# A two-layer encoder trunk: transposes through DRAM move to GpSimd's queue in runs of 512 bytes, and the last piece of y is transposed on TensorE

## The chip, the cores and the metric

The kernel runs on one core of one Trainium2 chip. The metric is the device time of one execution in microseconds, the median of several runs. The profile is one further execution, recorded instruction by instruction.

## The reference

Two identical layers act on x of 256 positions by 2048 channels, in float32. In each layer, with h the RMS-normalised input:

```python
u = h @ w_in                 # cq, ckv, kr, az | bq, bk, bv, bz | cq, ck, cv, cz | 3 gates of 2048
# A: latent attention; B: difference of two softmax maps per head; C: attention with a position bias
# q and k are normalised per head and multiplied by a gain; A and B rotate part of them
branches = (o_a * silu(a_z), o_b * silu(b_z), o_c * silu(c_z))      # 1024 channels each
y = sum(sigmoid(gate[n]) * (branches[n] @ w_branch[n]) for n in range(3))
x = x + y @ w_out
```

## The kernel before, in words

All products with weights go through one helper, `matunit` (L138 to L166). It multiplies a left side of 256 positions, stored transposed (channels on partitions), with 512 columns of a weight matrix. The weights come from DRAM as a stream in the order of use: chunks of 256 rows by 512 columns (512 KB), each loaded by SyncE (L153) into one of four buffers, cast on ScalarE to the high part (L154), and subtracted on VectorE to give the low part (L155). Each chunk feeds twelve TensorE matmuls: high by high, high by low and low by high, for two row blocks and two position blocks (L163 to L165). Four PSUM tiles hold two such products at a time.

An operand that was computed with positions on partitions has to be transposed before it can be a left side, and q, k and the branch outputs have to be transposed for attention and the branch projection. There are two ways. `to_transposed` (L199 to L213) uses TensorE: eight 128x128 transposes into PSUM for a piece of 512 channels, and then a split into high and low parts on ScalarE and VectorE, two halves of 128x512. `bounce` (L218 to L230) goes through DRAM. VectorE transposes 32x32 blocks of the piece in place (L223, two instructions), SyncE writes the piece to a DRAM tile (L225, 512 KB), and SyncE reads it back in four DMAs of 128 KB (L229), one for each quarter of the partitions, in runs of 32 floats (128 bytes), so that whole rows stand transposed afterwards. `from_bounced` (L232 to L241) then splits the result: ScalarE writes the high part times a gain, VectorE the low part. The variants `split_stacked` and `split_twice` place the parts of branch B's q and k on both halves of the partitions.

A `bounce` is used 42 times: for the normalised latent cq (once a layer), for the gated halves of A, B and C (six a layer), for q and k of the halves of B and C (eight a layer), for the four pieces of y (four a layer, L663), and for the four pieces of layer 1's input, in layer 0's output projection (L725). The gated halves of A and C are bounced before attention, and `simple_half` (L381 to L396) multiplies each head's output into the bounced tile (L395).

The order of a layer is: the latents, A in two halves, B in two halves, then the gates and the branch projection of A (`gate_branch(0)`), C in two halves, `gate_branch(1)` for B, `gate_branch(2)` for C, and the output projection. `gate_branch(2)` finishes y piece by piece (j = 0 to 3, L647 to L663), and the output projection reads all four pieces in each of its products (L712). Before it, GpSimd issues the load of the residual `xres` (2 MB, L703), whose buffer is that of `yacc`, the sum of y; in layer 0 GpSimd also issues the writes of the new x to DRAM (L721).

GpSimd computes the inverse roots of the norms (`rstd`, L245 and L246), the products behind them (L267, L424), and the rotary products of B's q and k and of A's shared key (L282 to L287, L552); it issues the loads of C's bias (L675). VectorE then scales and transposes what GpSimd has finished.

Every engine executes its instructions in order, and each queue of DMA issues is in order too. The order on each engine isn't written out by hand: a planner places the instructions of all engines by its own estimates of their times, starting from the order of the program. Two pools matter for the change: `zp` has four buffers of the tag z, for the gated halves and the tile that the pieces of y are read back to (L662), and `ps_t` has two PSUM buffers for transposes.

Of the kernel before, what the change touches and what calls it, by code (L numbers as in the profile page):

```python
# [14 lines left out]
P = 128  # L15
# [6 lines left out]
HH = 4  # L22
# [59 lines left out]
def trunk_kernel(ctx: ExitStack, tc: tile.TileContext, x, xT, w, cols, rows, tab, bias, ident_d, out):  # L82
# [106 lines left out]

    def split_twice(d0, d1, l0, l1, src, gain):  # L190

        a, b = slice(0, 64), slice(64, P)
        for hi, lo, d, dl in ((a, b, d0, l0), (b, a, d1, l1)):
            for o in (hi, lo):
                nc.scalar.activation(d[o], src[hi], AF.Copy, scale=gain[hi])
                nc.vector.scalar_tensor_tensor(out=dl[o], in0=src[hi], scalar=gain[hi],
                                               in1=d[hi].bitcast(F32), op0=ALU.mult, op1=ALU.subtract)

# [19 lines left out]
    def bounce(src, name, dst=None):  # L218


        dst = src if dst is None else dst
        for t in range(NT):
            nc.vector.transpose(dst[:, t, :], src[:, t, :])  # L223
        scr = dram.tile([SEQ, 512], F32, name=f"{name}_scr")
        nc.sync.dma_start(scr.rearrange("(t p) f -> p t f", p=P), dst)  # L225
        sv = scr.rearrange("(i r) (b j c) -> j r b i c", r=32, b=HH, j=4, c=32)
        flat = dst.rearrange("p t f -> p (t f)")
        for j in range(4):
            nc.sync.dma_start(flat[32 * j:32 * j + 32].rearrange("p (b i c) -> p b i c", b=HH, c=32), sv[j])  # L229
        return flat.rearrange("p (b q) -> p b q", b=HH)  # L230

    def from_bounced(z, dh, dl, gain, per_block=False, put=None):  # L232

        if put is not None:
            for b0 in (0, 2):
                put(slice(b0, b0 + 2), z[:, b0:b0 + 2, :])
        elif per_block:
            for b in range(HH):
                split(dh[:, b, :], dl[:, b, :], z[:, b, :], gain(b))
        else:  # L240
            split(dh, dl, z, gain)  # L241

# [138 lines left out]
    def simple_half(z, parts, v, add, name):  # L381

        zt = bounce(z, f"{name}zT")
        for hl in range(HH):
# [9 lines left out]
            o = attend_transposed(p, v, hl, n)  # L394
            nc.vector.tensor_tensor(out=zt[:, hl, :], in0=o[:, :SEQ], in1=zt[:, hl, :], op=ALU.mult)  # L395
        return zt  # L396
# [38 lines left out]
    for l in range(DEPTH):  # L435
# [135 lines left out]
        def b_split(z, hf, name, gain=None):  # L571
            bh[hf] = zp.tile([P, HH, SEQ], F32R, tag=f"bh{hf}", name=f"{name}h", bufs=1)
            bl[hf] = zp.tile([P, HH, SEQ], F32R, tag=f"bl{hf}", name=f"{name}l", bufs=1)
            split(bh[hf], bl[hf], z, gain)

# [35 lines left out]
        for hf in range(2):  # L611
            n = f"l{l}b{hf}"
            op = {}
            for i, nm in ((1, "k"), (0, "q")):
# [5 lines left out]
                if nm == "k":  # L620
                    d = [att_tile(f"{n}{nm}{m}") for m in range(2)]
                    put = lambda bs, pt: split_twice(d[0][:, 0, bs, :], d[1][:, 0, bs, :], d[0][:, 1, bs, :],
                                                     d[1][:, 1, bs, :], pt, cg[:, 4:5])
                else:
                    d = att_tile(f"{n}{nm}")
                    d = [d[:, 0], d[:, 1]]
                    put = lambda bs, pt: split_stacked(d[0][:, bs, :], d[1][:, bs, :], pt, cg[:, 1:2])
                from_bounced(bounce(nat, f"{n}{nm}T"), None, None, None, put=put)
                op[nm] = d
# [14 lines left out]
        def gate_branch(n):  # L644
            for j in range(4):
# [13 lines left out]
                if n == 2:  # L659
                    yt = att_tile(f"{nm}y")  # L660
                    yh[j], yl[j] = yt[:, 0], yt[:, 1]
                    yz = zp.tile([P, NT, 512], F32, tag="z", name=f"{nm}yz")  # L662
                    from_bounced(bounce(yacc[:, :, js], f"{nm}yT", yz), yh[j], yl[j], None)  # L663

# [140 lines left out]
```

## Time and profile before

| | us |
|---|---|
| median of 3 runs | 2031.13 |
| lowest and highest run | 2028.79, 2031.28 |
| the profiled execution: its own time | 2029.23 |
| the profiled execution: its span, first to last instruction | 2027.3 |

| engine | busy share of the span | instructions |
|---|---|---|
| TensorE matmul | 98% | 9112 |
| VectorE | 63% | 1750 |
| ScalarE | 55% | 1624 |
| GpSimd | 11% | 357 |

Times in the rows below are counted from the start of the span. PE is TensorE's matmul row, PEld its weight loads, DVE is VectorE, ACT ScalarE, POOL GpSimd, SP SyncE; a q behind the name is that engine's sequencer. A matmul's recorded length (0.39 us) overlaps the next one's, so the distance of their starts is read, not the length. PEclk is the granted share of the full TensorE clock. Names give layer and place: l0o is layer 0's output projection, l0n2j3y the last piece of y, l0b1q the q of B's second half. A tile that ends in `T_scr` is a bounce's tile in DRAM.

### The profile page before, as it was taken

Reading aid. Unit: us, or ns where it says so; the run is one execution under the profiler, and the core shown is the slowest. Engines: PE = TensorE matmul, PEld = TensorE weight load, DVE = VectorE, ACT = ScalarE, POOL = GpSimd, SP = SyncE. Lnnn points to the kernel's source line nnn. Section 1 sums busy time; section 2 is a strip of 40 time slices with the busy share of each in tenths; the row PEclk is TensorE's granted clock in tenths of the full one; section 3 lists DMA queues with packets and bytes.
Section 4 is the critical chain, followed back from the end, with each engine's and each line's share of the span. In section 5 each row is a group of like instructions: output and inputs, shape, how many; then the busy total and the mean of one; then the engine's idle time right before and its main releaser. Section 6 shows DMA issues by size and latency. Waiting matters only on the chain.

```text
span 2027.3 us, 25409 instructions
## 1 busy us (share of the span) xinstructions
PE 1985.4 (98%) x9112; PEld 1647.3 (81%) x9112; DVE 1267.4 (63%) x1750; ACT 1107.0 (55%) x1624; POOL 225.4 (11%) x357
## 2 busy tenths in 40 slices
PE   9999999999999999998999999999999999999989
PEld 7888778888888888887888887788888888888867
DVE  5778777545666555555657777775456665555544
ACT  6677667545555544443556766664456564444433
POOL 2313040001000000000023220400010100000000
PEclk9999999999999999999999999999999999999989
DMA  8765565666776656677886665756676676657774
GB/s 295 219 188 175 186 207 187 207 204 209 223 210 212 192 191 197 215 235 241 260 237 205 180 181 173 227 178 209 204 220 214 203 217 189 196 197 211 235 228 156
DMA packets 293325, 421.39 MB, mean 208 GB/s; under 512 B 187328, under 2 KB 191424, under 8 KB 292432
## 3 DMA queue, kind: packets, MB, share of 16 engines
q1 hardware_dynamic: 290992, 410.80, 65.4%
q0 software_dynamic: 1920, 8.46, 1.3%
q8 instruction: 71, 1.16, 0.2%
q14 instruction: 54, 0.44, 0.1%
q10 hardware_dynamic: 288, 0.52, 0.1%
HBM read 393.51 MB, written 26.21 MB: 207 GB/s over the span
## 4 chain that ended last, share of the span: by engine, by line
PE 77%; DMA 8%; ACT 4%; POOL 3%; DVE 3%; issue 3%; SPq 2%; ACTq 0%; POOLq 0%; DVEq 0%
PE l1g_p L164 4%; PE l1g_p L165 4%; PE l1g_p L163 4%; PE l0g_p L164 4%; PE l0g_p L165 4%; PE l0g_p L163 4%; SPq L229 2%; PE l1o_p L163 1%; PE l1o_p L165 1%; PE l1o_p L164 1%; PE l0o_p L164 1%; PE l0o_p L163 1%; PE l0o_p L165 1%; DMA l0cq_r<-w 1%; PE l1az_p L164 1%
## 5 line engine op out<-in xcount | busy, mean ns | idle before, releaser
L155 DVE TENSOR_TENSOR l1g_l<-l1g_r,l1g_h 128x1024 fp32r<-128x1024 f32 x96 | 117.3, 1222 | 94.4 <-ACT l1g_h L154 94.3
L155 DVE TENSOR_TENSOR l0g_l<-l0g_r,l0g_h 128x1024 fp32r<-128x1024 f32 x96 | 117.2, 1222 | 93.3 <-ACT l0g_h L154 93.2
L154 ACT CAST l0g_h<-l0g_r 128x1024 fp32r<-128x1024 f32 x96 | 101.1, 1053 | 130.0 <-PE l0g_p L165 79.8
L154 ACT CAST l1g_h<-l1g_r 128x1024 fp32r<-128x1024 f32 x96 | 101.1, 1054 | 127.8 <-PE l1g_p L165 78.1
L164 PE MATMUL l0g_p<-l0g_l,xh 128*128 128x512 f32 x384 | 149.8, 390 | 0.0
L165 PE MATMUL l0g_p<-l0g_h,xl 128*128 128x512 f32 x384 | 149.7, 390 | 0.0
L164 PE MATMUL l1g_p<-l1g_l,xh 128*128 128x512 f32 x384 | 149.7, 390 | 0.0
L165 PE MATMUL l1g_p<-l1g_h,xl 128*128 128x512 f32 x384 | 149.7, 390 | 0.0
L163 PE MATMUL l1g_p<-l1g_h,xh 128*128 128x512 f32 x384 | 136.0, 389 | 0.0
L163 PE MATMUL l0g_p<-l0g_h,xh 128*128 128x512 f32 x384 | 136.0, 390 | 0.0
L164 PEld LDWEIGHTS l0g_p<-l0g_l,xh 128*128 128x128 f32 x384 | 72.1, 188 | 15.3 <-DVE l0g_l L155 0.5
L164 PEld LDWEIGHTS l1g_p<-l1g_l,xh 128*128 128x128 f32 x384 | 72.1, 188 | 14.8
L165 PEld LDWEIGHTS l1g_p<-l1g_h,xl 128*128 128x128 f32 x384 | 72.1, 188 | 14.7
L165 PEld LDWEIGHTS l0g_p<-l0g_h,xl 128*128 128x128 f32 x384 | 72.1, 188 | 14.7
L163 PEld LDWEIGHTS l0g_p<-l0g_h,xh 128*128 128x128 f32 x384 | 72.1, 188 | 14.7
L163 PEld LDWEIGHTS l1g_p<-l1g_h,xh 128*128 128x128 f32 x384 | 72.0, 188 | 14.7
L155 DVE TENSOR_TENSOR l1o_l<-l1o_r,l1o_h 128x1024 fp32r<-128x1024 f32 x32 | 39.2, 1224 | 46.1 <-ACT l1o_h L154 46.1
L154 ACT CAST l1o_h<-l1o_r 128x1024 fp32r<-128x1024 f32 x32 | 33.7, 1054 | 58.5 <-PE l1o_p L165 45.6
L155 DVE TENSOR_TENSOR l0o_l<-l0o_r,l0o_h 128x1024 fp32r<-128x1024 f32 x32 | 38.8, 1219 | 29.5 <-ACT l0o_h L154 29.5
L154 ACT CAST l0o_h<-l0o_r 128x1024 fp32r<-128x1024 f32 x32 | 33.3, 1051 | 39.5 <-PE l0o_p L165 32.0
L703 POOL DMA_DIRECT2D xres<-x x1 | 0.8, 784 | 309.5 <-DVE l0n2j3yz L223 309.5
L703 POOL DMA_DIRECT2D xres<-xscr x1 | 0.8, 792 | 308.8 <-DVE l1n2j3yz L223 308.8
(1600 smaller groups left out, 5866.3 us busy)
## 6 DMA issues: line engine op xcount, KB each, us to landing
l0g_r<-w SPq DMA_DIRECT2D x96, 512.0 KB, 3.6
l1g_r<-w SPq DMA_DIRECT2D x96, 512.0 KB, 4.2
l0o_r<-w SPq DMA_DIRECT2D x32, 512.0 KB, 4.9
l1o_r<-w SPq DMA_DIRECT2D x32, 512.0 KB, 4.4
l0az_r<-w SPq DMA_DIRECT2D x16, 512.0 KB, 4.7
l1az_r<-w SPq DMA_DIRECT2D x16, 512.0 KB, 4.7
l0b0k_r<-w SPq DMA_DIRECT2D x8, 512.0 KB, 3.7
l0b0q_r<-w SPq DMA_DIRECT2D x8, 512.0 KB, 3.3
```

Source lines behind the costliest of these rows:

```text
L154: state["cast"] = nc.scalar.copy(wh[:, ks, :N], wr[:, ks, :N])
L155: nc.vector.tensor_tensor(out=wl[:, ks, :N], in0=wr[:, ks, :N], in1=wh[:, ks, :N].bitcast(F32), op=ALU.subtract)
L163: nc.tensor.matmul(ps[t][:, :N], h[:, ts], wh[:, k2, :N], start=first, stop=False)
L164: nc.tensor.matmul(ps[t][:, :N], h[:, ts], wl[:, k2, :N], start=False, stop=False)
L165: nc.tensor.matmul(ps[t][:, :N], lo[:, ts], wh[:, k2, :N], start=False, stop=last)
L229: nc.sync.dma_start(flat[32 * j:32 * j + 32].rearrange("p (b i c) -> p b i c", b=HH, c=32), sv[j])
L703: nc.gpsimd.dma_start(xres, x_src.rearrange("(t p) d -> p t d", p=P))
```

## The change

- `bounce` writes VectorE's transposes to a new tile `turned` (a z buffer), in an order in which the four channel blocks of a partition quarter lie together. The DRAM tile holds for each position row four runs of 128 floats, and the four reads fetch runs of 512 bytes. The write and the reads are issued by GpSimd.
- The bounced tile now has the order (position block, head, position in block). `bounced` and `as_bounced` are views that bring it and its targets together, in runs of 32 elements; the splits and the product in `simple_half` go through them.
- `from_bounced` multiplies by the gain in place, in a ScalarE pass of its own over the whole tile, and then splits without a gain; the case of one gain per block is as it was. `split_twice` loses its gain, and `split_stacked` is called without one. Both now take the whole tile at once and not two halves.
- In `gate_branch(2)`, the piece j = 3 goes through `to_transposed`, on TensorE.

```diff
--- before.py
+++ after.py
@@ -187,14 +187,13 @@
                 nc.vector.scalar_tensor_tensor(out=d[lo], in0=src[hi], scalar=gain[hi],
                                                in1=d[hi].bitcast(F32), op0=ALU.mult, op1=ALU.subtract)
 
-    def split_twice(d0, d1, l0, l1, src, gain):
+    def split_twice(d0, d1, l0, l1, src):
 
         a, b = slice(0, 64), slice(64, P)
         for hi, lo, d, dl in ((a, b, d0, l0), (b, a, d1, l1)):
             for o in (hi, lo):
-                nc.scalar.activation(d[o], src[hi], AF.Copy, scale=gain[hi])
-                nc.vector.scalar_tensor_tensor(out=dl[o], in0=src[hi], scalar=gain[hi],
-                                               in1=d[hi].bitcast(F32), op0=ALU.mult, op1=ALU.subtract)
+                nc.scalar.copy(d[o], src[hi])
+                nc.vector.tensor_tensor(out=dl[o], in0=src[hi], in1=d[hi].bitcast(F32), op=ALU.subtract)
 
     def to_transposed(src, nblk, dh, dl, gain, name, per_block=False, put=None):
 
@@ -218,27 +217,42 @@
     def bounce(src, name, dst=None):
 
 
+
+        turned = zp.tile([P, NT, 4, HH, 32], F32, tag="z", name=f"{name}_tu")
+        scr = dram.tile([NT, P, 4, 128], F32, name=f"{name}_scr")
+        for t in range(NT):
+            nc.vector.transpose(turned[:, t].rearrange("p j b c -> p b j c"), src[:, t, :])
+        nc.gpsimd.dma_start(scr.rearrange("t p j f -> p t (j f)"), turned.rearrange("p t j b c -> p t (j b c)"))
         dst = src if dst is None else dst
-        for t in range(NT):
-            nc.vector.transpose(dst[:, t, :], src[:, t, :])
-        scr = dram.tile([SEQ, 512], F32, name=f"{name}_scr")
-        nc.sync.dma_start(scr.rearrange("(t p) f -> p t f", p=P), dst)
-        sv = scr.rearrange("(i r) (b j c) -> j r b i c", r=32, b=HH, j=4, c=32)
         flat = dst.rearrange("p t f -> p (t f)")
+        sv = scr.rearrange("t (i r) j f -> j r (t i) f", r=32)
         for j in range(4):
-            nc.sync.dma_start(flat[32 * j:32 * j + 32].rearrange("p (b i c) -> p b i c", b=HH, c=32), sv[j])
-        return flat.rearrange("p (b q) -> p b q", b=HH)
+            nc.gpsimd.dma_start(flat[32 * j:32 * j + 32].rearrange("p (q f) -> p q f", f=128), sv[j])
+        return flat
+
+    def bounced(z, b=None):
+
+        v = z.rearrange("p (q b c) -> p q b c", b=HH, c=32)
+        return v if b is None else v[:, :, b, :]
+
+    def as_bounced(d):
+
+        if len(d.shape) == 2:
+            return d.rearrange("p (q c) -> p q c", c=32)
+        return d.rearrange("p b (q c) -> p q b c", c=32)
 
     def from_bounced(z, dh, dl, gain, per_block=False, put=None):
 
+        if per_block:
+            for b in range(HH):
+                split(as_bounced(dh[:, b, :]), as_bounced(dl[:, b, :]), bounced(z, b), gain(b))
+            return
+        if gain is not None:
+            nc.scalar.activation(z, z, AF.Copy, scale=gain)
         if put is not None:
-            for b0 in (0, 2):
-                put(slice(b0, b0 + 2), z[:, b0:b0 + 2, :])
-        elif per_block:
-            for b in range(HH):
-                split(dh[:, b, :], dl[:, b, :], z[:, b, :], gain(b))
+            put(bounced(z), as_bounced)
         else:
-            split(dh, dl, z, gain)
+            split(as_bounced(dh), as_bounced(dl), bounced(z))
 
     def rstd(ss, n, width, name):
 
@@ -392,7 +406,8 @@
                 pc = p[:, 0:P] if t == 0 else p[:, P:384]
                 nc.scalar.activation(pc, pc, AF.Copy, scale=su[:, t:t + 1])
             o = attend_transposed(p, v, hl, n)
-            nc.vector.tensor_tensor(out=zt[:, hl, :], in0=o[:, :SEQ], in1=zt[:, hl, :], op=ALU.mult)
+            zc = bounced(zt, hl)
+            nc.vector.tensor_tensor(out=zc, in0=as_bounced(o[:, :SEQ]), in1=zc, op=ALU.mult)
         return zt
 
     def diff_half(z, parts, v, nlam, name):
@@ -571,7 +586,7 @@
         def b_split(z, hf, name, gain=None):
             bh[hf] = zp.tile([P, HH, SEQ], F32R, tag=f"bh{hf}", name=f"{name}h", bufs=1)
             bl[hf] = zp.tile([P, HH, SEQ], F32R, tag=f"bl{hf}", name=f"{name}l", bufs=1)
-            split(bh[hf], bl[hf], z, gain)
+            from_bounced(z, bh[hf], bl[hf], gain)
 
         za = [None, None]
         qr = [None, None]
@@ -619,13 +634,12 @@
                     rope(v, v, rt[:, t, c0:c0 + 16], rt[:, t, c0 + 16:c0 + 32], 8, 8, nc.gpsimd, f"{n}{nm}r{t}")
                 if nm == "k":
                     d = [att_tile(f"{n}{nm}{m}") for m in range(2)]
-                    put = lambda bs, pt: split_twice(d[0][:, 0, bs, :], d[1][:, 0, bs, :], d[0][:, 1, bs, :],
-                                                     d[1][:, 1, bs, :], pt, cg[:, 4:5])
+                    put = lambda pt, v: split_twice(v(d[0][:, 0]), v(d[1][:, 0]), v(d[0][:, 1]), v(d[1][:, 1]), pt)
                 else:
                     d = att_tile(f"{n}{nm}")
                     d = [d[:, 0], d[:, 1]]
-                    put = lambda bs, pt: split_stacked(d[0][:, bs, :], d[1][:, bs, :], pt, cg[:, 1:2])
-                from_bounced(bounce(nat, f"{n}{nm}T"), None, None, None, put=put)
+                    put = lambda pt, v: split_stacked(v(d[0]), v(d[1]), pt)
+                from_bounced(bounce(nat, f"{n}{nm}T"), None, None, cg[:, 1:2] if i == 0 else cg[:, 4:5], put=put)
                 op[nm] = d
             v = vsplit(in_unit(f"b{hf}v"), rcol, f"{n}v")
             zb[hf] = silu_gate(in_unit(f"b{hf}z"), rcol, f"{n}z")
@@ -659,8 +673,11 @@
                 if n == 2:
                     yt = att_tile(f"{nm}y")
                     yh[j], yl[j] = yt[:, 0], yt[:, 1]
-                    yz = zp.tile([P, NT, 512], F32, tag="z", name=f"{nm}yz")
-                    from_bounced(bounce(yacc[:, :, js], f"{nm}yT", yz), yh[j], yl[j], None)
+                    if j < 3:
+                        yz = zp.tile([P, NT, 512], F32, tag="z", name=f"{nm}yz")
+                        from_bounced(bounce(yacc[:, :, js], f"{nm}yT", yz), yh[j], yl[j], None)
+                    else:
+                        to_transposed(lambda t: yacc[:, t, js], 4, yh[j], yl[j], None, f"{nm}yT")
 
         gate_branch(0)
         for hf in range(2):
```

## Rows read from the trace of the kernel before

**Rows 1.** Busy time of the engines, page.

```profile
PE 1985.4 (98%) x9112; PEld 1647.3 (81%) x9112; DVE 1267.4 (63%) x1750; ACT 1107.0 (55%) x1624; POOL 225.4 (11%) x357
```

**Rows 2.** A window in the gates; length, then busy us (instructions) by engine.

```profile
700.00:915.00 215.00, 215.00 (x950) 177.93 (x949) 119.66 (x117) 97.92 (x101) 0.00 (x0) 1.00 0.66 207
```

**Rows 3.** TensorE's waits: total us, times, longest us.

```profile
PE l1o_p L163 <- ACT l1n2j3y L171: 8.0, 1, 8.0
PE l0o_p L163 <- ACT l0n2j3y L171: 6.1, 1, 6.1
PE l0b1v_p L163 <- ACT l0b1v_h L154: 2.4, 1, 2.4
PE l0c_s L311 <- ACT l0c1q L174: 1.6, 1, 1.6
PE l0b0z_p L163 <- ACT l0b0z_h L154: 1.6, 1, 1.6
PE l1b0z_p L163 <- ACT l1b0z_h L154: 1.5, 1, 1.5
...
PE l1az_p L163 <- ACT l1az_h L154: 0.9, 1, 0.9
```

**Rows 4.** Windows behind long waits; third column from the right is the granted clock.

```profile
302.00:305.40 3.40, 3.40 (x9) 2.61 (x10) 2.65 (x3) 0.00 (x0) 0.00 (x0) 0.50 0.55 86
942.30:947.10 4.80, 4.80 (x11) 3.79 (x12) 2.33 (x2) 1.05 (x1) 0.00 (x0) 0.50 0.79 287
1220.20:1227.00 6.80, 6.48 (x16) 5.02 (x17) 6.26 (x15) 2.77 (x6) 0.00 (x0) 0.50 0.48 147
1949.90:1954.00 4.10, 4.10 (x10) 3.23 (x11) 2.32 (x2) 1.03 (x1) 0.00 (x0) 0.50 0.75 272
```

**Rows 5.** The chain that ended last: start us, us, what.

```profile
109.62 0.87 PE l0a0kT_t L205 x8
...
923.02 1.31 DVE l0n2j3yz L223 x2
```

**Rows 6.** Timeline of ScalarE in both output projections; idle time before it in brackets.

```profile
930.81 1.05 ACT L154 CAST l0o_h<-l0o_r 128x1024 fp32r<-128x1024 f32 x1 [1.67 <-PE l0o_p L165]
934.63 1.05 ACT L154 CAST l0o_h<-l0o_r 128x1024 fp32r<-128x1024 f32 x1 [2.76 <-DMA l0o_r<-w]
...
1943.68 1.04 ACT L154 CAST l1o_h<-l1o_r 128x1024 fp32r<-128x1024 f32 x1 [6.17 <-DMA l1o_r<-w]
```

**Rows 7.** Line L229, the reads: issue ns min/median/max.

```profile
L229 SPq DMA_DIRECT2D x1n<-x1T_scr x16: 562/672/2798, 957.4 to 1026.5; - x16
```

**Rows 8.** The chain that ended last, around two read-backs.

```profile
204.68 1.33 SPq L229
...
207.72 4.63 DMA l0b0z_r<-w
...
1048.17 3.04 SPq L229
1053.20 6.34 DMA l1az_r<-w
```

**Rows 9.** Line L721, the writes of x that GpSimd issues: ns min/median/max.

```profile
L721 POOL DMA_DIRECT2D xscr<-xres x4: 727/727/760, 951.4 to 1017.1; - x4
```

**Rows 10.** A window in branch B's second half; the fifth engine is GpSimd.

```profile
271.00:296.10 25.10, 25.10 (x112) 20.79 (x111) 19.57 (x25) 13.41 (x17) 20.64 (x29) 1.00 0.81 234
```

**Rows 11.** DMA issues: queue, count, KB each, median us from issue to landing.

```profile
xscr<-xres POOLq DMA_DIRECT2D x4, 512.0 KB, 4.8
x1T_scr<-x1n SPq DMA_DIRECT2D x4, 512.0 KB, 5.0
```

**Rows 12.** The chain that ended last, a split of C's q.

```profile
629.33 1.16 ACT l0c1q L174
```

**Rows 13.** Timeline of GpSimd in the rotary products of B's second half.

```profile
277.83 0.32 POOL L285 TENSOR_TENSOR l0b1kr_b<-l0b1k_n,rt 128x64 f32<-128x64 f32 x1
...
279.47 1.32 POOL L285 TENSOR_TENSOR l0b1kr_b<-l0b1k_n,rt 128x64 f32<-128x64 f32 x1
```

## The prediction

> **What bounds the kernel now.** I read the page's busy time first: TensorE is busy for 98% of the span [rows 1]. In an undisturbed stretch 950 matmuls take 215 us, 0.226 us each [rows 2], so nearly all the time is matmul issue, which this change hardly touches. Only the holes in TensorE's row can be won or lost, so the second view is the list of TensorE's waits [rows 3]. Two stand apart: each layer's output projection (L163, l0o_p and l1o_p) waits 6.1 and 8.0 us for ScalarE's split of the last piece of y, which has come back from DRAM. The others are 2.4 us or less. Third, the windows with the granted clock [rows 4]: after both long waits TensorE ran at 0.50, the 1.2 GHz level, for 11 matmuls in 4.80 us and 10 in 4.10 us; the same level stands after the l1b0z wait and around the l0b1v wait. Fourth, I asked what ends the short waits.
>
> **The last piece of y.** It leaves the DRAM round trip: no transposes on VectorE, no write, no four reads, no wait for them. Removed are the two waits, 6.1 + 8.0 = 14.1 us, and the matmuls at the lower level: 4.80 - 11 x 0.226 = 2.3 us and 4.10 - 10 x 0.226 = 1.8 us, together 4.1 us [rows 3, 4]. Added are eight TensorE transposes a layer: a group of eight takes 0.87 us, so 1.7 us for both layers [rows 5]. Their source is ready at 923.02, when the old way's VectorE transposes start [rows 5]; TensorE went on at 942.3 after 6.1 us of waiting, so it wants the piece at 936.2, 13 us later. The split, now two halves each on ScalarE and VectorE, has its cover there. Net so far -16.5 us.
>
> **What is late next there: weights.** While the last piece travels, the residual (xres, 2 MB, issued by GpSimd) is loading. A ScalarE cast of a weight chunk normally idles 1.67 us before it, waiting for TensorE; one cast in each layer idled 2.76 and 6.17 us instead, for its weights [rows 6]. These were 1.1 and 4.5 us short, hidden so far by the longer wait for y. Casts run ahead of their matmuls, so not all of these 5.6 us would reach TensorE: I take half, +2.8. Lower end 0, because the write and reads that shared the weights' queue are gone; upper end 9 us and the clock loss of 4.1 us again, because TensorE no longer pauses and drains weights at full rate while xres loads.
>
> **What SyncE loses.** All other round trips (40 of 42) move to GpSimd's queue, each one write and four reads. On SyncE a read issue takes 0.67 us, at most 2.80 [rows 7], and the reads wait for the write to land, with weight loads queued behind. The chain of waits shows it: reads at 204.68 and 1048.17, the next weight chunk issued only at 207.72 and 1053.20, and TensorE then waits for it [rows 8]. These waits are l0b0z 1.6, l1b0z 1.5 and l1az 0.9 us [rows 3], and after l1b0z some 3.2 us of lower clock (half of the 6.48 us busy [rows 4]); 7.2 us in all. The round trip itself stays, and ScalarE and VectorE still wait for it ahead of their next casts; so I take half, -3.6 us, with ends 0 and -7.2.
>
> **What GpSimd gains.** An issue there costs about 0.73 us (the write of 512 KB in 256 runs [rows 9]); the new read has 256 runs too (32 partitions by 8 pieces of 512 bytes, where the old one had 1024 of 128), so five issues cost 3.7 us per round trip. Queued behind them and behind the wait for the write are the inverse roots and the rotary products of the next q or k (L245 to L287), and VectorE's transpose and ScalarE's casts wait for those. In most stretches GpSimd is idle (11% of the span busy [rows 1]) and I price the move at nothing; cover gone, it would be the rival below. The second half of branch B is different: from 271 to 296 us GpSimd is busy 20.64 of 25.10 us [rows 10], and two round trips (b0z and b1k) fall into it. Ten issues are 7.3 us against 4.5 us free, so 2.8 us a layer, +5.6 us. Lower end 0 (the planner of the engines' orders puts other work in front of TensorE), upper end the rival's 14.2 us a layer.
>
> **Latency of a round trip.** Write and reads from GpSimd land much as from SyncE: 4.8 us for xscr against 5.0 for x1T_scr, the same size [rows 11]. Longer runs can only help, and the read issues of up to 2.80 us were SyncE's; the added ScalarE pass that multiplies the piece by its gain costs 1.16 us, by the equal pass at 629.33 [rows 12]. There are 20 such passes (16 for q and k, 4 for branch B's output): 23 us on an engine that is 55% busy. They lie on a path only where scores wait for q, as in l0c_s (1.6 us [rows 3]), four times. I take 0, with ends -2.1 x 4 = -8.5 us (the worst read issue against the usual one [rows 7]) and +4.6 us. In exchange the B splits run as half as many instructions of twice the length.
>
> **Other edits.** Splits, the gate product and the transposes now walk 32-element pieces. No row shows that; the same instructions on whole rows are the nearest, so I take 0, and 0.7 us more per transpose as the upper end, which is off TensorE's path except at the four score waits (+5.6). The `turned` tile takes one of four z slots until the write has landed; two gated halves beside it leave a free slot, so 0; were it gone, VectorE's queue would stand. Layer 1's input pieces are issued behind the xscr writes on GpSimd, 0.73 us later each [rows 9], and the product that uses them comes to the last piece last: 0, at worst +0.7.
>
> **A rule against the change.** In the trace, a GpSimd product that takes 0.32 us took 1.32 us at 279.47 [rows 13]. GpSimd's DMA issues do not show this: 0.727 to 0.760 us, four times [rows 9]. The Trainium skill's page "SBUF — State Buffer" (section "SBUF: two separate sides") says that a VectorE instruction in a two-port mode locks GpSimd out of a shared port, so that a DMA issued by GpSimd waits for its descriptors, and advises the other queues. The issue rows disagree with that for this kernel's VectorE instructions, so the sum holds no term for it; it is a rival.
>
> **Sum.** -14.1 - 4.1 + 1.7 + 2.8 - 3.6 + 5.6 = -11.7 us. The profiled execution took 2029.23 us (span 2027.3 and 1.9 around it), 1.9 under the median of the runs, 2031.13, and within their spread. 2029.23 - 11.7 = 2017.5, so 2018 us.
>
> **Rivals.**
> 1. GpSimd takes the place of SyncE as the queue that holds the weights up, and the kernel gets slower. Place: the second half of B in each layer. Ten issues, 7.3 us, and two waits for a write of 5.0 us each [rows 11], less 4.5 us free: 12.8 us, and 1.4 us of lower clock as after l0b1v (9 matmuls in 3.40 us [rows 4]): 14.2 us a layer, 28.4 in place of 5.6. -11.7 + 22.8 = +11.1: 2040 us. It decides from 8.6 us a layer on, where it uses up the other terms (17.3 us). For it: TensorE already waits 2.4 us for l0b1v there, with VectorE behind GpSimd. Against it: other GpSimd work can be put into the waits.
> 2. Weights starve beside xres, and most of the old wait comes back: 9 us and the clock's 4.1 us in place of 2.8. -11.7 + 10.3 = -1.4: 2028 us, no change. For it: the 6.17 us cast [rows 6]. Against it: part of that chunk's delay was the write ahead of it in its queue.
> 3. GpSimd's issues find room everywhere, SyncE's blocked loads all vanish, and xres costs nothing: -14.1 - 4.1 + 1.7 - 7.2 = -23.7: 2005.5 us. For it: no weight load waits for a DRAM write any more.
> 4. VectorE holds up GpSimd's issues by 1.0 us each, the difference in [rows 13]: 20 issues in the two stretches of B, -11.7 + 20 = +8.3: 2038 us. This is what that page's rule would do here; the issue rows speak against it.
> 5. The change doesn't do what it says for the last piece: the orders of all engines are planned anew, and the transposes stand so late in TensorE's order that a wait of the old size remains: 2030 us.
>
> **How the numbers follow.** Forecast 0.54 (by itself 2010 to 2024), rival 1 0.12, rival 2 0.11, rival 3 0.16, rival 4 0.04, rival 5 0.03. About 0.2%, 4 us, is what a measurement of this kernel can tell from no change. Faster: forecast and rival 3, 0.70. Same: rivals 2 and 5, 0.14. Slower: rivals 1 and 4, 0.16. The range reaches from a little under rival 3 to rival 2 and 5, 2003 to 2030, and leaves out the slower cases.
>
> **What would show it.** Right: no TensorE wait on the split of the last y piece, granted clock 1.00 at the start of both projections, casts there that wait for weights at most some 3 us, no weight load behind a round trip in SyncE's waits, GpSimd's stretch in B some 3 us longer. Wrong: TensorE waits of over 5 us in B's second half whose chain runs through GpSimd's issues or a write's landing (rival 1); a cast of the projection that idles over 5 us on weights (rival 2); GpSimd issues of 1.7 us (rival 4). A new wait at the latent projections, where GpSimd's norms of the key latents share the queue with the cq round trip, would be one that I have not priced.

## The result, and the profile after

The change made the kernel slower by 1%: median 2049.66 us (2048.69 to 2055.04, 4 runs) against 2029.96 us for the kernel before on the same chip, a ratio of 1.0107 with a 95% interval of 1.0082 to 1.0131. The forecast of 2018 us and its range are missed, on the wrong side. The profiled execution of the changed kernel took 2049.82 us, 20.6 us more than the one that stands ahead of the prediction.

The page of the changed kernel, first the busy time [rows 1], then the packets and the two largest DMA queues (packets, MB, share of 16 engines):

```profile
PE 1997.7 (98%) x9128; PEld 1650.8 (81%) x9128; DVE 1258.4 (61%) x1724; ACT 1118.3 (55%) x1624; POOL 349.3 (17%) x557
...
DMA packets 120622, 419.30 MB, mean 205 GB/s; under 512 B 15136, under 2 KB 19232, under 8 KB 119728
...
q1 hardware_dynamic: 104848, 366.75, 55.0%
q0 software_dynamic: 15360, 50.41, 8.9%
```

GpSimd is busier, 17% against 11%, and ScalarE has much the same work as before. The round trips have moved: the queue of GpSimd (q0) carries 50 MB now.

TensorE's largest waits in the changed kernel (total us, times, longest us), the answer to [rows 3]:

```profile
PE l0b1z_p L163 <- ACT l0b1z_h L154: 3.7, 1, 3.7
PE l0c1v_p L163 <- ACT l0c1v_h L154: 3.2, 1, 3.2
PE l0o_p L163 <- ACT l0o_h L154: 2.6, 2, 1.7
PE l1b1z_p L164 <- DVE l1b1z_l L155: 2.4, 2, 2.0
PE l1c1v_p L163 <- ACT l1c1v_h L154: 2.2, 1, 2.2
```

The two waits for the last piece of y, 8.0 and 6.1 us, are gone. In their place are many waits of 1 to 4 us, and what TensorE waits for in most of them is a weight cast of ScalarE (`_h`, L154) or the VectorE instruction behind it (`_l`, L155). Two windows of the changed kernel, one at the last piece of y and one behind the wait for l0c1v (columns as in [rows 4]):

```profile
1955.00:1965.00 10.00, 10.00 (x50) 8.35 (x49) 7.08 (x9) 4.81 (x6) 0.72 (x1) 1.00 0.61 188
628.96:632.40 3.44, 3.44 (x9) 2.70 (x10) 2.83 (x5) 1.04 (x2) 3.19 (x4) 0.50 0.41 152
```

At the last piece TensorE keeps the full clock (1.00); behind l0c1v it runs at 0.50, the 1.2 GHz level, as it did behind the long waits before.

What is late is seen on ScalarE. Its timeline in the changed kernel where the k of C's second half comes back (start us, us, instruction, in brackets the idle time and who ended it):

```profile
616.26 1.05 ACT L154 CAST l0c1v_h<-l0c1v_r 128x1024 fp32r<-128x1024 f32 x1 [1.67 <-PE l0c1q_p L165]
622.88 1.15 ACT L251 ACTIVATE l0c1k_n<-l0c1k_n,colt 128x1024 f32<-128x1024 f32 x1 [5.57 <-DMA l0c1k_n<-l0c1kT_scr]
623.94 0.56 ACT L268 COPY l0c1q_n<-l0c1q_p 128x512 f32<-128x512 f32 x1
624.41 1.04 ACT L171 CAST l0c1k<-l0c1k_n 128x1024 fp32r<-128x1024 f32 x1
625.35 0.58 ACT L268 COPY l0c1q_n<-l0c1q_p 128x512 f32<-128x512 f32 x1
625.83 0.73 ACT L275 ACTIVATE l0c1q_sq<-l0c1q_n,rcol 128x512 f32<-128x512 f32 x1
626.46 1.04 ACT L154 CAST l0c1v_h<-l0c1v_r 128x1024 fp32r<-128x1024 f32 x1
```

ScalarE stands idle for 5.57 us in front of the gain pass (L251), which waits for the reads to land. The next weight cast, at 626.46, is behind it in the order, and TensorE waits 3.2 us for that cast. The cast's turn, 2.72 us after the one at 616.26, was 618.98, so it came 7.5 us late; an estimate from these numbers is that it could have come some 4 us late before TensorE felt it. I add up all such idle time of ScalarE in front of instructions that the landing of a read released: 95.8 us in the kernel before, 111.1 us in the changed one, although two round trips are gone.

The round trip itself is longer. From the end of VectorE's second transpose to the landing of the last read, the median is 11.0 us over the 42 round trips before and 13.9 us over the 40 after. The time from issue to landing of a read (min, median, max) in the changed kernel:

```profile
DMA to landing us min/median/max: 2.6/4.9/8.8
```

Before, the same line had a median of 3.9 us. So my first theory was that GpSimd's queue, with its longer round trip, was the whole loss. Rival a was the separate gain pass, rival b the layout.

### The profile page after: what moved, and what is told of

Read it like the earlier page. It is cut to its first block, busy times and chain, and to the rows that moved or that the text cites. A ratio compares the mean times of both kernels' runs of the same rounds, so it can differ in the third digit from the quotient of the medians.

```text
span 2047.9 us, 25486 instructions
## 1 busy us (share of the span) xinstructions
PE 1997.7 (98%) x9128; PEld 1650.8 (81%) x9128; DVE 1258.4 (61%) x1724; ACT 1118.3 (55%) x1624; POOL 349.3 (17%) x557
## 5 line engine op out<-in xcount | busy, mean ns | idle before, releaser
L155 DVE TENSOR_TENSOR l0g_l<-l0g_r,l0g_h 128x1024 fp32r<-128x1024 f32 x96 | 117.2, 1222 | 95.5 <-ACT l0g_h L154 95.4
L155 DVE TENSOR_TENSOR l1g_l<-l1g_r,l1g_h 128x1024 fp32r<-128x1024 f32 x96 | 117.1, 1222 | 95.3 <-ACT l1g_h L154 95.2
L154 ACT CAST l0g_h<-l0g_r 128x1024 fp32r<-128x1024 f32 x96 | 101.1, 1055 | 130.2 <-PE l0g_p L165 82.5
L154 ACT CAST l1g_h<-l1g_r 128x1024 fp32r<-128x1024 f32 x96 | 101.2, 1055 | 129.8 <-PE l1g_p L165 82.5
L155 DVE TENSOR_TENSOR l1o_l<-l1o_r,l1o_h 128x1024 fp32r<-128x1024 f32 x32 | 39.2, 1225 | 41.6 <-ACT l1o_h L154 41.6
L154 ACT CAST l1o_h<-l1o_r 128x1024 fp32r<-128x1024 f32 x32 | 33.8, 1055 | 53.2 <-PE l1o_p L165 48.2
L155 DVE TENSOR_TENSOR l0o_l<-l0o_r,l0o_h 128x1024 fp32r<-128x1024 f32 x32 | 38.8, 1220 | 28.2 <-ACT l0o_h L154 28.2
L154 ACT CAST l0o_h<-l0o_r 128x1024 fp32r<-128x1024 f32 x32 | 33.3, 1050 | 38.6 <-PE l0o_p L165 32.0
```

The lines of the kernel that those rows point to most:

```text
L154: state["cast"] = nc.scalar.copy(wh[:, ks, :N], wr[:, ks, :N])
L155: nc.vector.tensor_tensor(out=wl[:, ks, :N], in0=wr[:, ks, :N], in1=wh[:, ks, :N].bitcast(F32), op=ALU.subtract)
```

## The experiments

Each ratio is to the kernel before on the same chip. The chips differ: the kernel before took 2023.83 to 2029.96 us on them, so kernels are best compared by their ratios. "Places" says behind which weight cast ScalarE's passes over returned pieces stand; "idle" is ScalarE's idle time for landings, added up as above, from the profiled execution.

| run | queue | runs, bytes | gain pass | last y | places | median us | ratio to before, 95% | idle us |
|---|---|---|---|---|---|---|---|---|
| changed kernel | GpSimd | 512 | yes | TensorE | planner's | 2049.66 | 1.0107 (1.0082 to 1.0131) | 111.1 |
| e1_y_only | SyncE | 128 | no | TensorE | planner's | 2013.78 | 0.9932 (0.9920 to 0.9945) | 89.5 |
| e2_sync512 | SyncE | 512 | yes | TensorE | planner's | 2051.06 | 1.0123 (1.0103 to 1.0142) | 136.0 |
| e3_gain_in_split | GpSimd | 512 | no | TensorE | planner's | 2070.50 | 1.0210 (1.0193 to 1.0228) | 116.4 |
| e4_pool128 | GpSimd | 128 | no | DRAM | planner's | 2084.06 | 1.0282 (1.0263 to 1.0300) | 133.0 |
| e5_late512 | SyncE | 512 | yes | TensorE | as in e1 | 2003.23 | 0.9893 (0.9878 to 0.9908) | 48.8 |
| e6_early128 | SyncE | 128 | no | TensorE | as in e2 | 2050.15 | 1.0134 (1.0114 to 1.0154) | 127.7 |
| e7_gain128 | SyncE | 128 | yes | TensorE | as in e1 | 2010.41 | 0.9935 (0.9919 to 0.9951) | 85.2 |
| e8_late_pool | GpSimd | 512 | yes | TensorE | later | 2021.65 | 0.9985 (0.9975 to 0.9996) | 50.7 |
| e9_later512 | SyncE | 512 | yes | TensorE | as in e8 | 2003.43 | 0.9884 (0.9862 to 0.9906) | 12.7 |
| e10_late512b | SyncE | 512 | yes | TensorE | e5, one moved | 2006.28 | 0.9893 (0.9874 to 0.9912) | 55.4 |
| e11_bpass_pool | GpSimd | 512 | yes | TensorE | four moved | 2053.87 | 1.0127 (1.0102 to 1.0153) | 106.6 |
| e12_later128 | SyncE | 128 | yes | TensorE | as in e8 | 2003.23 | 0.9884 (0.9866 to 0.9902) | 19.8 |

### One part alone

**e1_y_only.** The kernel before with the hunk in `gate_branch(2)` alone.

```diff
-                    yz = zp.tile([P, NT, 512], F32, tag="z", name=f"{nm}yz")
-                    from_bounced(bounce(yacc[:, :, js], f"{nm}yT", yz), yh[j], yl[j], None)
+                    if j < 3:
...
+                    else:
+                        to_transposed(lambda t: yacc[:, t, js], 4, yh[j], yl[j], None, f"{nm}yT")
```

> The kernel before with one edit: the last piece of y transposed on TensorE. Main theory (the y edit gained what was forecast, and the round trips through GpSimd's queue lost more than that): 2013 us, some 17 us under before, since both layers lose their two waits of 7 us in the output projection and nothing else moves; range 2008 to 2019. Rival (the transposes themselves or the new order of the output projection are what costs): 2030 us or more.

Measured: 2013.78 us, 14.0 us under the kernel before (2027.76 us on the same chip). The y edit is a gain, and the rest of the change has lost more than twice as much.

**e2_sync512.** The changed kernel, its DMAs on SyncE.

```diff
-        nc.gpsimd.dma_start(scr.rearrange("t p j f -> p t (j f)"), ...
+        nc.sync.dma_start(scr.rearrange("t p j f -> p t (j f)"), ...
...
-            nc.gpsimd.dma_start(flat[32 * j:32 * j + 32] ...
+            nc.sync.dma_start(flat[32 * j:32 * j + 32] ...
```

> The changed kernel with its write and its four reads issued by SyncE again; the 512-byte layout, the separate gain pass and the y edit stay. Main theory (the queue is the loss: the round trip takes 13.9 us from GpSimd's queue and 11.0 from SyncE's): the median round trip falls to 11 us or under and the time to 2013 to 2022 us. Rival a (the gain pass of 1.15 us on ScalarE ahead of each split, and its place in ScalarE's order) and rival b (the layout): the time stays at 2040 us or above.

Measured: 2051.06 us. My theory fell: the median round trip did shorten, to 9.6 us, and nothing came back. ScalarE waited for landings longer than in any other run of the study, 136.0 us, with one of the shortest round trips. That can only be if it came to wait earlier.

**e3_gain_in_split.** The changed kernel without the separate pass; VectorE takes one scaled instruction per head.

```diff
-        if gain is not None:
-            nc.scalar.activation(z, z, AF.Copy, scale=gain)
...
+        elif gain is not None:
+            nc.scalar.activation(as_bounced(dh), bounced(z), AF.Copy, scale=gain)
+            stt_heads(as_bounced(dl), bounced(z), gain, as_bounced(dh))
```

> The changed kernel with the gain back in the splits, so that no separate pass over the piece runs on ScalarE; VectorE's part of a scaled split becomes one instruction per head. GpSimd's queue, the 512-byte layout and the y edit stay. Main theory (the queue is the loss): some 5 to 10 us come back, 2040 to 2045 us, and the round trips stay near 13.9 us. Rival a (the gain pass is the loss): 2015 to 2025 us.

Measured: 2070.50 us, 21 us more than the changed kernel. Both theories expected a gain. The edit changed ScalarE's order too, so it tells little of the pass itself; e7 below does.

**e4_pool128.** The kernel before, its write and reads on GpSimd's queue and nothing else.

```diff
-        nc.sync.dma_start(scr.rearrange("(t p) f -> p t f", p=P), dst)
+        nc.gpsimd.dma_start(scr.rearrange("(t p) f -> p t f", p=P), dst)
...
-            nc.sync.dma_start(flat[32 * j:32 * j + 32] ...
+            nc.gpsimd.dma_start(flat[32 * j:32 * j + 32] ...
```

> The kernel before with one edit: the write and the four reads of the round trip issued by GpSimd, in 128-byte runs as before, no gain pass, the last piece of y by round trip. Main theory (the queue is the loss): slower than before by 20 to 35 us, 2050 to 2065 us, with round trips of 14 us or more. Rivals a and b (the gain pass, the layout): within 5 us of 2030 us.

Measured: 2084.06 us, 56 us slower, more than the 20 to 35 us expected, with a median round trip of 15.4 us. So the queue does cost, but e2 shows that taking it away doesn't help by itself. Something common to both had to be found.

### The place in ScalarE's order

I counted weight casts on ScalarE ahead of each pass. In e1 the pass over the q and k of C and the pieces of y stands behind three casts from the end of the transposes; in e2 behind two; in the changed kernel behind four. In a product these casts start 2.72 us apart, so one place is 2.72 us. ScalarE's timeline in e1 and then in e9 below, at the same k of C as above:

```profile
607.84 1.15 ACT L174 ACTIVATE l0c1k<-l0c1k_n,colt 128x1024 fp32r<-128x1024 f32 x1 [2.86 <-DMA l0c1k_n<-l0c1kT_scr]
608.90 1.04 ACT L154 CAST l0c1v_h<-l0c1v_r 128x1024 fp32r<-128x1024 f32 x1
```

```profile
605.29 1.05 ACT L158 CAST l0c1v_h<-l0c1v_r 128x1024 fp32r<-128x1024 f32 x1
606.25 1.15 ACT L258 ACTIVATE l0c1k_n<-l0c1k_n,colt 128x1024 f32<-128x1024 f32 x1
607.30 0.71 ACT L282 ACTIVATE l0c1q_sq<-l0c1q_n,rcol 128x512 f32<-128x512 f32 x1
607.91 1.04 ACT L158 CAST l0c1v_h<-l0c1v_r 128x1024 fp32r<-128x1024 f32 x1
```

In e1 the split waits 2.86 us and the cast comes behind it. In e9 the casts go first and nothing waits. The new theory: what costs is not the length of the round trip but ScalarE reaching the pass before its data are there. Any edit to the round trip lets the planner choose another place, and that place decides. The next kernels hold the places fixed, with the same mechanism in all of them:

```diff
+    later = {}
+    def behind(key, fn):
+        later.setdefault(key, []).append(fn)
...
+            for fn in later.pop((name, c), ()):
+                with tc.issue_after(state["cast"].ins):
+                    fn()
...
-                from_bounced(bounce(nat, f"{n}{nm}T"), th[:, 0], th[:, 1], ...
+                zt, gn = bounce(nat, f"{n}{nm}T"), ...
+                behind((f"{n}v", 0) if nm == "k" else (f"{n}z", 0),
+                       lambda zt=zt, th=th, gn=gn: from_bounced(zt, th[:, 0], th[:, 1], gn))
```

The second hunk stands in `matunit`, behind the cast of chunk c of the product `name`; the key says which. The same is done for B's q and k, the pieces of y and layer 1's input; the gain passes of B's gated halves stand behind `gate_branch(0)`, where their splits are. The planner still may go later: in e5 the passes over B's q stand one or two casts later than in e1. The 71 us in the next expectation is too low; by the count of the table e1 has 89.5 us.

**e5_late512.** e2 with this, and the keys as above.

> The run with 512-byte runs on SyncE (e2_sync512), with only the order on ScalarE changed: its passes over a piece that has come back are held behind the same weight casts as in e1_y_only, one cast later than the planner put them in most places, and the gain passes of branch B's gated halves stand behind the branch projection of A. New main theory (the planner expects the 512-byte round trip back earlier and puts ScalarE's pass one cast, 2.7 us, further ahead; ScalarE then waits in order, 136 us in all against 71, and the weight casts behind it come late): the time falls from 2051 to 2014 to 2024 us. Rivals a and b (the gain pass itself, the layout itself): 2040 us or more.

Measured: 2003.23 us, 48 us under e2 (47 us by the ratios), some 8 us under e1 by the ratios, and lower than expected, with the layout, the gain pass and SyncE's queue untouched.

**e6_early128.** e1 with keys that aim at the places of e2, and the next cast held behind the split. For C, y and the input pieces they are one chunk earlier than in e5; in B the keys of the first half are not earlier.

```diff
-                state["cast"] = nc.scalar.copy(wh[:, ks, :N], wr[:, ks, :N])
+                held = state.pop("hold", None)
+                with ExitStack() as st:
+                    if held is not None:
+                        st.enter_context(tc.issue_after(held.ins))
+                    state["cast"] = nc.scalar.copy(wh[:, ks, :N], wr[:, ks, :N])
...
+                behind((f"{n}q", 7) if nm == "k" else (f"{n}v", 7), ...
```

> The other way round: the kernel of e1_y_only (128-byte runs on SyncE, no gain pass) with ScalarE's splits of q, k, y and the input pieces held to the earlier places that they have in e2_sync512, each ahead of the next weight cast. New main theory (the place in ScalarE's order): 2035 to 2055 us against 2014, ScalarE's waits for round trips at 120 us or more. Rivals a and b: 2010 to 2020 us, since nothing of the layout or of the gain pass is in it.

Measured: 2050.15 us, 36 us over e1 (41 us by the ratios), with the old layout, the old queue and no gain pass. ScalarE's timeline in e6, where the q of C's second half comes back:

```profile
626.18 1.05 ACT L162 CAST l0c1v_h<-l0c1v_r 128x1024 fp32r<-128x1024 f32 x1 [1.67 <-PE l0c1v_p L176]
633.73 1.15 ACT L185 ACTIVATE l0c1q<-l0c1q_n,cgain 128x1024 fp32r<-128x1024 f32 x1 [6.50 <-DMA l0c1q_n<-l0c1qT_scr]
634.79 1.03 ACT L162 CAST l0c1z_h<-l0c1z_r 128x1024 fp32r<-128x1024 f32 x1
```

From one cast to the next 8.6 us pass, where 2.72 us is the pace. All of TensorE's waits for a weight cast or for the VectorE instruction behind it come to 16.0 us in e1 and 43.4 us in e6. The mean granted clock falls from 0.997 to 0.990, which makes, as an estimate, 12 and 41 us at the lower level, where the windows behind the two long waits before [rows 4] show 0.41 to 0.44 us a matmul and not 0.226. Together e5 and e6 show the place to be what moved the time between e1 and e2, in both directions.

**e7_gain128.** e1 with the gain pass of the changed kernel, at e1's places.

```diff
+        if gain is not None:
+            nc.scalar.activation(z, z, AF.Copy, scale=gain)
...
-            split(dh, dl, z, gain)
+            split(dh, dl, z)
```

> The kernel of e1_y_only with a separate ScalarE pass for the gain, as in the changed kernel, and with ScalarE's passes held at the places of e1_y_only. Rival a (the gain pass of 1.15 us, 20 times, is the loss): 2035 us or more. New main theory: 2014 to 2022 us, at most the four waits of scores for q longer by 1.15 us each.

Measured: 2010.41 us; by the ratios to before the same as e1 (0.9935 and 0.9932). Rival a falls: the pass costs nothing beyond the interval of some 3 us. The places aren't quite e1's: by the count above, five of B's passes stand one cast later and three of C's one earlier.

### The queue and the layout at fixed places

**e8_late_pool.** The changed kernel, held. By the count above, C's passes and most of B's stand one or two casts later than the planner had put them, the gain passes of B's gated halves far later; the pieces of y, and on the whole those of layer 1's input, stay where they were.

```diff
+                behind((f"{n}v", 2) if nm == "k" else (f"{n}z", 3), ...
...
+                        behind((f"l{l}g2{j + 1}", 7), ...
```

> The changed kernel, with everything on GpSimd's queue as it is, and ScalarE's passes held one or two casts later than the planner put them. New main theory: most of the loss comes back, 2020 to 2032 us, the rest being round trips of 13.9 us that scores wait for; ScalarE's waits for round trips fall from 111 to under 50 us. If the queue itself is the loss (GpSimd's norms and rotary products held up behind the issues): 2040 us or more.

Measured: 2021.65 us, with 50.7 us of idle. Most of the loss came back, without a change to any DMA.

**e9_later512.** e8 with the write and the reads on SyncE (the edit of e2).

> The kernel of e8_late_pool with its write and reads issued by SyncE, ScalarE's passes at the same places: the queue alone. If the queue costs little once the places leave room for its longer round trip: within 6 us of e8_late_pool, 2015 to 2025 us. If GpSimd's queue costs by itself (its norms and rotary products behind the issues, in B above all): 2000 to 2012 us, with the gain in B's second half and at the input of layer 1.

Measured: 2003.43 us, some 20 us under e8 by the ratios. At equal places the queue does cost. GpSimd's timeline in e8, in the second half of B:

```profile
284.23 0.72 POOL L232 DMA_DIRECT2D l0b1kT_scr<-l0b1kT_tu  x1 [1.04 <-DVE l0b1kT_tu L231]
285.74 0.19 POOL L266 TENSOR_SCALAR l0b1q_ss<-l0b1q_ss 128x8 f32<-128x8 f32 x1 [0.79 <-DVE l0b1q_ss L283]
286.01 1.67 POOL L267 TENSOR_TENSOR l0b1q_ss<-l0b1q_ss,mhalf 128x8 f32<-128x8 f32 x1
287.76 0.20 POOL L266 TENSOR_SCALAR l0b1q_ss<-l0b1q_ss 128x8 f32<-128x8 f32 x1
292.63 2.37 POOL L237 DMA_DIRECT2D l0b1k_n<-l0b1kT_scr  x4 [4.67 <-DMA l0b1kT_scr<-l0b1kT_tu]
295.02 0.21 POOL L288 TENSOR_TENSOR l0b1q_ss<-l0b1q_ss,rcol 128x8 f32<-128x8 f32 x1
...
301.39 0.46 POOL L308 TENSOR_TENSOR l0b1q_n<-l0b1qr_a,l0b1qr_b 128x128 f32<-128x128 f32 x1
```

The same last product of the rotary in e9:

```profile
296.11 0.47 POOL L308 TENSOR_TENSOR l0b1q_n<-l0b1qr_a,l0b1qr_b 128x128 f32<-128x128 f32 x1
```

GpSimd waits 4.67 us for the write to land and spends 2.37 us on four read issues, so the reads of k land late. What they hold up is ScalarE again. The pass over k stands behind the last cast of v in both kernels. ScalarE's timeline in e8, and TensorE's wait for the cast at 305.92 (total us, times, longest us):

```profile
300.47 1.15 ACT L258 ACTIVATE l0b1k_n<-l0b1k_n,cgain 128x1024 f32<-128x1024 f32 x1 [4.25 <-DMA l0b1k_n<-l0b1kT_scr]
301.65 4.25 ACT L202 CAST l0b1k<-l0b1k_n 64x1024 fp32r<-64x1024 f32 x4
305.92 1.99 ACT L158 CAST l0b1z_h<-l0b1z_r 128x1024 fp32r<-128x1024 f32 x2
```

```profile
PE l0b1z_p L170 <- ACT l0b1z_h L158: 3.6, 1, 3.6
```

Layer 1 has the same, 3.1 us on ScalarE and 2.5 on TensorE. The pass in e9, 3.9 us after its reads have landed:

```profile
298.63 1.14 ACT L258 ACTIVATE l0b1k_n<-l0b1k_n,cgain 128x1024 f32<-128x1024 f32 x1
```

The norms of q stand behind GpSimd's wait and issues too, and q is ready 5.3 us later than in e9. No cost of that shows: the pass over q starts 5.6 us after its reads have landed.

Set against e9, TensorE in e8 falls back 5.7 us over that half of B in layer 0 and 5.8 us in layer 1. The rest of the 19.7 us at the end comes in C (6.1 and 3.5 us, where VectorE's product with a gated half waits for late reads) and at the joint of the layers (3.4 us), less 4.8 us by which e8 is ahead in A and in B's first half. The median round trip is 13.3 us in e8 and 9.6 us in e9. The Trainium skill's page "DMA: Bandwidth & Descriptors" (section "SWDGE vs HWDGE vs iDMA") calls the path of DMAs from SyncE or ScalarE faster to set up than GpSimd's. These runs agree: the issue of a read takes 0.45 us on SyncE in e9 and 0.58 us on GpSimd in e8 (medians).

**e12_later128.** e7 with the places of e8, so that the layout alone differs from e9.

> The kernel of e7_gain128 (128-byte runs on SyncE, the gain in a pass of its own) with ScalarE's passes at the later places of e9_later512: the layout alone, at places that leave room for either round trip. If the longer runs help only by coming back sooner (10 us against 11): 2003 to 2007 us, as e9_later512, since a place that late no longer waits for either. If the 128-byte packets cost by themselves (SyncE's longer issues, the weights behind them): 2009 to 2016 us.

Measured: 2003.23 us, ratio 0.9884, as e9. The median round trip is 11.2 us, longer than e9's, and TensorE doesn't wait for the difference (its waits come to 15.9 us in all, and to 15.6 in e9). Rival b falls: once the passes stand late enough, 512-byte runs neither cost nor gain. At the earlier keys, where ScalarE still waits, they do gain: by their edits e5 and e7 differ in the layout alone, and e5 is some 8 us faster by the ratios, with round trips of 9.4 against 10.7 us and 48.8 against 85.2 us of idle.

### Two that missed

**e10_late512b.** e5 with the key for the k of B's first half one chunk later.

```diff
-                behind((f"{n}v", 0 if hf == 0 else 5) if nm == "k" else (f"{n}z", 1),
+                behind((f"{n}v", 1 if hf == 0 else 5) if nm == "k" else (f"{n}z", 1),
```

> The kernel of e5_late512 with one place moved: the pass for k of B's first half stands one cast later in each layer, where ScalarE waited 3.3 and 3.1 us and TensorE 1.4 us with 3.4 us at the lower clock behind it. Main theory (a wait of ScalarE ahead of a weight cast is what TensorE feels): 3 to 6 us less, 1997 to 2000 us. If these waits are felt elsewhere anyway: 2003 us again.

Measured: 2006.28 us, the same ratio as e5. The idle time became more (55.4 us), not less. The planner placed other passes anew: ScalarE's waits for this k went from 3.3 and 3.1 us to 3.4 and 1.5, those for the q behind it from 2.4 and 1.4 to 4.7 and 4.6. So the run doesn't show what one such wait is worth.

**e11_bpass_pool.** The changed kernel with the gain passes of B's gated halves held behind the branch projection of A.

```diff
-            from_bounced(z, bh[hf], bl[hf], gain)
+            with tc.issue_after(state["cast"].ins):
+                from_bounced(z, bh[hf], bl[hf], gain)
```

> The changed kernel with one edit: the gain passes of branch B's gated halves, which the planner put some 60 casts ahead of their splits and which ScalarE waited for 4.7, 2.5, 4.5 and 4.0 us, stand behind the branch projection of A. Main theory: 6 to 14 us less than the changed kernel, 2036 to 2044 us. If these passes only use idle time: 2047 us or more.

Measured: 2053.87 us, no better than the changed kernel; the idle time fell by only 4.5 us. The four waits are gone, but others grew, those ahead of the k of B's second half from 4.3 and 2.0 to 6.8 us each. Moving these four passes alone brings nothing back.

## Why the prediction was wrong

**The last piece of y: right; the weights beside it: too high.** The steps of the first came to -16.5 us, and with the weights -13.7; e1 measured -14.0, which by its interval (11 to 16 us) hardly tells the two apart. The traces do: from the last product into y to the end of the output projection, e1 takes 6.6 us less than the kernel before in layer 0 and 9.4 us less in layer 1, 16.0 in all. The waits are gone and the clock holds at 1.00. "What is late next there", +2.8 us, hardly came: in layer 0 of the changed kernel a cast waits 2.23 us for its weights, and no wait of TensorE follows it; in e1 TensorE has only a wait of 0.5 us left in both output projections. That -13.7 lies so near to -14.0 is partly luck.

**The step that failed** is "Latency of a round trip", where I took 0 with ends of -8.5 and +4.6 us. It rests on the sentence that the passes "lie on a path only where scores wait for q", four times. That overlooked the order on ScalarE: a pass that waits for a landing holds every weight cast behind it, and TensorE lives on those casts. I took a busy share of 55% for cover, and did not ask what stands ahead of a cast in the order. ScalarE idles 1.67 us ahead of a cast [rows 6], and the waits in front of the passes are up to 6.1 us. The kernel before showed it: the 2.4 us wait for l0b1v_h [rows 3] is for a cast that stands behind the split of k, and that split waits for its landing:

```profile
292.65 2.96 ACT L195 ACTIVATE l0b1k<-l0b1k_n,cgain 64x512 fp32r<-64x512 f32 x4 [1.12 <-DMA l0b1k_n<-l0b1kT_scr]
295.93 2.94 ACT L195 ACTIVATE l0b1k<-l0b1k_n,cgain 64x512 fp32r<-64x512 f32 x4 [0.33 <-DMA l0b1k_n<-l0b1kT_scr]
298.90 1.99 ACT L154 CAST l0b1v_h<-l0b1v_r 128x1024 fp32r<-128x1024 f32 x2
```

Rival 1 put that wait down to VectorE behind GpSimd. With the step fell the claim that write and reads from GpSimd "land much as from SyncE" [rows 11]: that row was a large write, and the round trip went from 11.0 to 13.9 us.

The spans of the profiled executions split the 36.0 us from e1 (2011.9) to the changed kernel (2047.9): 27.0 for passes placed too early (changed kernel less e8, 2020.9), 19.7 for the queue (e8 less e9, 2001.2), less 10.7 that the later places win over e1 (e9 less e1). The split depends on the order in which the steps are taken: with the places as the planner chose them, the queue's part is nothing (e2 against the changed kernel) and the places' is 47 us (e5 against e2). So the step that I took as 0, at most +4.6 us, cost 27 us by the one order and 47 by the other.

**"What SyncE loses" and "What GpSimd gains"** came to +2.0 us together and were mis-sized: with the later places held, the move costs 20 us. Rival 1 had a place right, the second half of B, and where the delay starts, GpSimd's wait for the write. But it was given 0.12, it is 6 us a layer there and not 14, what TensorE waits for is a cast behind ScalarE's pass over k and not the work behind the norms, and it is not confined to that place. What would have shown it, waits in B's second half, came as 3.7 us, not the 5 us that I named. **"Other edits"**, taken as 0, held: e9 and e12 agree.

**Rival 4** did not happen: GpSimd's issues for the round trips took 0.58 to 0.81 us in the changed kernel, so the rule of the Trainium skill's page "SBUF — State Buffer" (section "SBUF: two separate sides") stays without a row that shows it here. **Rival 5** asked for a new order in the wrong place: the orders were planned anew, but it was ScalarE's that hurt.

What stays open: why the planner chose other places. That its estimate of a 512-byte round trip is shorter would fit e2, but no run here shows its estimates. It also planned the other engines anew in every kernel, so what their orders add to the 20 and 27 us isn't separated. Why a read from GpSimd's queue lands 1.6 us later than the same read from SyncE at equal places (5.9 against 4.35 us from the issue of the last read to its landing, medians of e8 and e9) was not tested either.

## What to carry to other kernels

Where engines run in order, price a transfer not by its length but by where its consumer stands: an instruction that waits for a landing holds all that is behind it, and shortening the transfer can make this worse if the order is planned anew. So after any such edit count what stands ahead of the consumer, and hold it behind enough independent work before judging the edit. The y edit and later passes, with layout and queue as before (e12, which has the gain pass besides), gave 2003 us, 1.2% under the kernel before.

## What was not expected of the hardware

- Runs of 128 and of 512 bytes made no difference to the time at the later places (e12 and e9, both 0.9884), though the round trips took 11.2 and 9.6 us.
- Here the queue decided how runs became packets. In e4 GpSimd's queue moved the round trips in 128-byte runs, yet the page counts few small packets:

```profile
DMA packets 121294, 421.40 MB, mean 202 GB/s; under 512 B 15296, under 2 KB 19392, under 8 KB 120400
...
q0 software_dynamic: 16032, 52.51, 11.0%
```

In the kernel before, the same bytes went from SyncE as part of 293325 packets, 187328 of them under 512 bytes. The larger packets did not arrive sooner: a read's median from issue to landing was 6.3 us in e4 and 3.9 us before.
